# Gate tiles between the pool pairs, an earlier weight block in the last scan group, and single PSUM banks for one product

## The chip, the core and the metric

The kernel runs on one NeuronCore of a Trainium2 chip. The metric is the device time of one execution in microseconds (us). The engines are PE (TensorE, matrix products; PEld is its weight load), DVE (VectorE, elementwise), ACT (ScalarE, elementwise and activation functions), POOL (GpSimd, here only for issuing DMAs) and SP (which issues most DMAs from its queue). Matrix products are written to PSUM, an accumulator memory of eight banks of 128 x 512 floats; all other on-chip data lie in SBUF.

## The reference

One layer of a decoder trunk on 512 tokens with 16 meta tokens ahead of them, model width 1024. Cut to what the change touches:

```python
u = rmsnorm(h, mix_norm_w)                      # 528 x 1024
proj = u @ w_in
gates = sigmoid(proj[..., OFF_GATE:] + b_gate)  # 2 x 1024 columns
gate_pool, gate_ssd = gates[..., :1024], gates[..., 1024:]
y_pool = pool_mixer(u_pool, pool_w_group, pool_scale) @ w_pool_up
y_ssd = mamba2_branch(z, xbc, dt_raw, ...) @ w_ssd_out
h = h + (gate_pool * y_pool + gate_ssd * y_ssd) @ w_o
v = rmsnorm(h, mlp_norm_w)
h = h + square(relu(v @ w_ff1)) @ w_ff2
out = rmsnorm(h, final_norm_w)
```

`pool_mixer` takes, in four groups of 256 channels, the mean over the last 2, 4, 8 or 16 positions minus the value itself, multiplies each group by a 256 x 256 matrix and scales it. `mamba2_branch` is a chunked scan in eight groups of 256 channels.

## The kernel before

Precision. The float32 products are made of products in a reduced format: each factor is split into a high part (a cast on ACT) and a low part (original minus high, on DVE), and three products are added in PSUM: high x high, high x low, low x high. `block()` loads one weight block of 128 x 1024 from a packed array (through one of three `raw` buffers), casts it to `whi` (L87) and subtracts to `wlo` (L88); there are four buffers of each. `mm3s` (L119, L120, L122) makes the three products of a list of factor pairs: first, pair by pair, high weight with high and low data, then the low weights. `proj` (L183, L185) does the same for eight pieces of 128 rows of `w_in`.

Order. Each engine works through its own queue in a fixed order, set when the program is built: a planner models the time and gives each engine, of the instructions whose inputs it takes to be ready, the one that was written earliest. So a step written earlier has precedence, and a step can be drawn ahead of others to fill a gap in the modelled time. `tc.issue_after(x)` holds an instruction behind x on its engine. The planner also deals out buffers: `psum2` takes one of two buffers of two banks (pool `psa`), `psum1` one of four single banks (pool `psb`). Weight blocks are loaded in the order in which `_weight_blocks` packs them, which must match the order in which the kernel asks for them.

The scan. `ssd(g)` handles scan group g as a generator of steps: transposes and the differences for the decay mask (L496 on ACT, L499 on DVE); chunk states `st` (L519 to L529) and the masked decay `abc` (exponentials L502, L503 on ACT, mask L530 on DVE); for each half the outputs `po` (state part) and `py` (masked part), and the DVE work on y (L546 to L550); squares; the norm; the final scaling with the split of y into `yh` and `yl` (L571, L572). `weave` alternates these steps with those of other generators. For the last group, g = 7, the other generator is `out_part`, which multiplies y of groups 4 to 6 (`ys[8]` to `ys[13]`) by pieces of `w_ssd_out` into `psp` and adds the sum to `acc` (L647). `PARTS` gives its order: for output tiles d = 0 and 1 first k = 8 to 11, later k = 12 and 13 (which come from group 6, the group just finished), then d = 2 to 7 whole. Its weights come by a generator `pieces` that gets a block (L634, L636) when its first piece is asked for; block 0 serves the first parts of d = 0 and 1, block 1 the late parts of both and the first four pieces of d = 2.

The pool branch. Behind the scan, `pool_tile` computes the two tiles of pool group 3; then eight products `psl` (k = 14, 15, the last group's y) are added to `acc` (L814 to L817); then comes one gate tile of the pool branch (`gate_pool(NK - 1)`). Pool groups 2, 1 and 0 are each computed by `pool_pair(p)` (L735 to L784): seven products of a split-matrix scheme with four weight forms A, S, D, B made from two raw blocks on DVE (sums L741 to L745, splits L105 and L106), into `pxx` (two banks), `py` and `pz` (single banks). `averaged` (L714) takes the windowed means on DVE, `pooled_halves` (L726) splits them, and `pool_mix(g)` multiplies by the group matrix into `pg`, scales and splits into `yph`, `ypl` (L796, L797). A pair is written ahead of the mix of the pair before.

The merge. For each of the eight output tiles d in the order of `MERGE`, `gate_ssd(d)` computes a gate tile (24 matmuls into `pgs`, a sigmoid L805 into one of two `gt` buffers); the product `pup` multiplies the pooled parts by `w_pool_up` (L926); `acc` is multiplied by the gate (L927) and the products added. Before the change the first gate tile is written behind pair 0 and in front of the mix of group 0; in the merge loop each turn first makes the gate tile of the next turn.

Of the kernel before, what the change touches and what calls it, by code (L numbers as in the profile page):

```python
# [9 lines left out]
F32 = mybir.dt.float32  # L10
F32R = mybir.dt.float32r
AF = mybir.ActivationFunctionType
ALU = mybir.AluOpType

P = 128
D = 1024
SEQ = 512
# [3 lines left out]
NK = D // P  # L21
G = 8
# [35 lines left out]
def kernel(ctx: ExitStack, tc, xT, x, w, vec, fnw, out):  # L58
# [12 lines left out]
    def block_tiles():  # L71
        b = nblk[0]
        nblk[0] += 1
        return (b, wp.tile([P, 1024], F32, tag="raw", name=f"raw{b}", bufs=3),
                wp.tile([P, 1024], F32R, tag="whi", name=f"whi{b}"),
                wp.tile([P, 1024], F32R, tag="wlo", name=f"wlo{b}"))

    def block_load(t, c):
        nc.sync.dma_start(t[1][:, c], w[t[0], :, c])
# [36 lines left out]
    def mm3s(ps, pairs, first=True, last=True):  # L116

        for n, ((ah, al), (bh, bl)) in enumerate(pairs):
            pe.matmul(ps, ah, bh, start=first and n == 0, stop=False)  # L119
            pe.matmul(ps, ah, bl, start=False, stop=False)  # L120
        for n, ((ah, al), (bh, bl)) in enumerate(pairs):
            pe.matmul(ps, al, bh, start=False, stop=last and n == len(pairs) - 1)  # L122
# [39 lines left out]
    def psum2(name):  # L162
        return psa.tile([P, 1024], F32, tag="mm", name=name)
# [51 lines left out]
    b = nblk[0]  # L215
# [409 lines left out]

    def out_part():

        def pieces():
            for n in range(6):
                t = block_tiles()  # L630
                block_load(t, slice(0, 1024))

                with tc.issue_after(b_meta[G - 1].ins) if n == 1 else nullcontext():
                    act.copy(t[2], t[1])  # L634
                with tc.issue_after(x_decayed[G - 1].ins) if n == 1 else nullcontext():
                    dve.tensor_tensor(t[3], t[1], t[2].bitcast(F32), op=ALU.subtract)  # L636
                for j in range(NK):
                    c = slice(j * P, (j + 1) * P)
                    yield t[2][:, c], t[3][:, c]

        un, ps = pieces(), {}
        for d, ks in PARTS:
            if d not in ps:
                ps[d] = psum2(f"psp{d}")[:, :SEQ]
            mm3s(ps[d], [(next(un), ys[k]) for k in ks], ks[0] == 8, ks[-1] == 13)
            if ks[-1] == 13:
                dve.tensor_tensor(acc[d], acc[d], ps[d], op=ALU.add)  # L647
            yield


# [135 lines left out]
    def pool_mix(gi, pooled, wgb):  # L786
        ps = [psum1(f"pg{gi}_{j}") for j in range(2)]
        wh, wl = wgb
        for j in range(2):
            os = [(gi % 2) * 512 + k * 256 + j * P for k in range(2)]  # L790
            mm3s(ps[j], [((wh[:, o : o + P], wl[:, o : o + P]), pooled[k]) for k, o in enumerate(os)])
        for j in range(2):
            t = 2 * gi + j
            h = yp.tile([P, SEQ], F32R, tag="yh", name=f"yph{t}")
            l = yp.tile([P, SEQ], F32R, tag="yl", name=f"ypl{t}")
            act.activation(h, ps[j], AF.Copy, scale=col(V_PS, t))  # L796
            dve.scalar_tensor_tensor(l, ps[j], col(V_PS, t), h.bitcast(F32),  # L797
                                     op0=ALU.mult, op1=ALU.subtract)
            yps[t] = (h, l)
# [12 lines left out]

    un = units()
    for d in range(NK):  # L814
        ps = psum2(f"psl{d}")[:, :SEQ]
        mm3s(ps, [(next(un), ys[k]) for k in (14, 15)])
        dve.tensor_tensor(acc[d], acc[d], ps, op=ALU.add)  # L817
    wgb = block()
    gate_pool(NK - 1)
    for n, gi in enumerate(POOL_ORDER):  # L820
        if n == 0:
            pool_mix(gi, pend, wgb)
            nxt = pool_pair(POOL_ORDER[1])
            continue
        pend, nxt = nxt, pool_pair(POOL_ORDER[n + 1]) if n < 3 else None
        if n == 2:
            wgb = block()
        if n == 3:
            gts = [gate_ssd(MERGE[0])]

        pend = [pooled_halves(*a, copied[POOL_ORDER[n + 1]] if n < 3 else None) for a in pend]
        with tc.issue_after(last[POOL_ORDER[n + 1]].ins) if n < 3 else nullcontext():
            pool_mix(gi, pend, wgb)
    pool_stack.close()
    wo_stack = ExitStack()
    wop = wo_stack.enter_context(tc.tile_pool(name="wop", bufs=1, side="right", reuse_waits="tile"))
# [77 lines left out]
    ks = [2 * gi + i for gi in POOL_ORDER for i in range(2)]  # L914
    first = []
    for n, d in enumerate(MERGE):
        if n + 1 < NK:
            gts.append(gate_ssd(MERGE[n + 1]))
        if n >= NK - 2:
            first.append(split(woq["b11", n - NK + 2]))  # L920
        ps = psum2(f"pup{d}")[:, :SEQ]
        wh, wl = block()
        if n < len(WO_ORDER):
            wo_load(*WO_ORDER[n])
        cs = [slice(k * P, (k + 1) * P) for k in ks]
        mm3s(ps, [((wh[:, c], wl[:, c]), yps[k]) for c, k in zip(cs, ks)])  # L926
        dve.tensor_tensor(acc[d], acc[d], gts[n], op=ALU.mult)  # L927
        dve.tensor_tensor(m1[d], m1[d], ps, op=ALU.mult)
        dve.tensor_tensor(acc[d], acc[d], m1[d], op=ALU.add)
        factors(d)  # L930
# [325 lines left out]
def _weight_blocks(i):  # L1256

    w_in, w_g, w_up = i["w_in"][0], i["pool_w_group"][0], i["w_pool_up"][0]
    w_so, w_o, f1, f2 = i["w_ssd_out"][0], i["w_o"][0], i["w_ff1"][0], i["w_ff2"][0]
    blocks = []  # L1260

    def cols(m, c):
        a = m[:, c : c + P]
        return a.reshape(NK, P, P).transpose(1, 0, 2).reshape(P, NK * P)

    def put(b):
        blocks.append(b)

    wdt = w_in[:, OFF_DT : OFF_DT + HEADS].reshape(NK, P, HEADS).transpose(1, 0, 2).reshape(P, NK * HEADS)
    put(np.concatenate([wdt, np.zeros((P, 1024 - NK * HEADS), wdt.dtype)], 1))  # L1270

    def group(g, gate_d=None):
        for t in (16 + g, 24 + g, 2 * g, 2 * g + 1):
            put(cols(w_in, OFF_XBC + t * P))
        if gate_d is not None:
            gate(gate_d)
        for j in range(2):
            put(cols(w_in, OFF_Z + (2 * g + j) * P))

    def wg(b):  # L1280
        put(w_g[2 * b : 2 * b + 2].reshape(2, 2, P, 256).transpose(2, 0, 1, 3).reshape(P, 1024))

    def gate(d):
        put(cols(w_in, OFF_GATE + d * P))

    def pieces(parts):

        u = [w_so[k * P : (k + 1) * P, d * P : (d + 1) * P] for d, ks in parts for k in ks]
        return [np.concatenate(u[j : j + NK], 1) for j in range(0, len(u), NK)]

    group(0)
    for d in range(GATES_FIRST):
        gate(d)
    for g in range(G - 1):
        if g == 4:
            for d in range(NK):
                put(cols(w_so[:D], d * P))
        group(g + 1, GATE_AT.get(g))
    blocks += pieces(PARTS)
    for t in range(2):  # L1300
        put(cols(w_in, (2 * POOL_ORDER[0] + t) * P))
    blocks += pieces([(d, (14, 15)) for d in range(NK)])
    wg(POOL_ORDER[0] // 2)
    gate(NK - 1)
    for n in range(4):
        for k in ((1, 2) if n == 0 else (n + 2,) if n == 1 else ()):
            for i in range(2):
                put(cols(w_in, (2 * POOL_ORDER[k] + i) * P))
        if n == 3:
            gate(NK + MERGE[0])  # L1310
        if n == 2:
            wg(POOL_ORDER[n] // 2)

    def wo(name, i):
        put(rows(w_o, 2 * (name[1] == "2") + i, int(name[2] == "2")))

    def rows(m, k2, half):
        a = m[k2 * 2 * P : (k2 + 1) * 2 * P, half * 512 : (half + 1) * 512]
        return a.reshape(2, P, 512).transpose(1, 0, 2).reshape(P, 1024)

    for n, d in enumerate(MERGE):
        if n + 1 < NK:
            gate(NK + MERGE[n + 1])
        put(cols(w_up, d * P))
        if n < len(WO_ORDER):
            wo(*WO_ORDER[n])
    for i in range(2):
        wo("b21", i)

    def quarter(c, k, half):  # L1330

        a = [f2[(4 * c + 2 * p + k) * P : (4 * c + 2 * p + k + 1) * P, half * 512 : (half + 1) * 512]
             for p in range(2)]
        return np.concatenate(a, 1)

    def quarters(c):
        for k, half in ((1, 0), (1, 1), (0, 1), (0, 0)):
            put(quarter(c, k, half))

    ff = list(range(32))  # L1340

    def ff1():
        if ff:
            put(cols(f1, ff.pop(0) * P))

    for _ in range(6):
        ff1()
    for c in range(8):
        quarters(c)
        for _ in range(3 if c > 4 else 4):  # L1350
            ff1()
    return np.ascontiguousarray(np.stack(blocks))
# [38 lines left out]
```

## Time and profile before

| | us |
|---|---|
| median of 3 runs | 1017.9 (1017.82 to 1017.94) |
| profiled execution | 1017.53 |
| its span, first to last instruction | 1015.8 |
| PE busy in the span | 1004.9 |
| DVE busy | 763.5 |
| ACT busy | 561.7 |

Times in timelines are microseconds from the start of the span. A row of a timeline has the start, the duration, the engine, the line, the operation, what is written and read, the shape, and the number of instructions merged into the row; idle time of the engine ahead of it and what ended it stand in brackets. A row of the waits has the engine and line that waited, the engine and line that ended the wait, the total in us, the number of times and the longest. In the busy time by stage each row has the window, its length, then for PE, PEld, DVE, ACT and POOL the busy time and the number of instructions, then the granted PE clock, the share of DMA and the rate. The matmuls are pipelined: one row of a 512-column product lasts 0.39 us, while the next one starts 0.23 us after it.

### The profile page before, as it was taken

How to read it: one execution, taken by the hardware profiler on the slowest of the kernel's cores; microseconds unless marked ns; L12 is line 12 of the kernel's file. 1: busy time of each engine (PE TensorE's matmuls, PEld its weight loads, DVE VectorE, ACT ScalarE, POOL GpSimd, SP SyncE). 2: the span in 40 equal slices, each digit the busy share in tenths (PEclk: the TensorE clock that was granted, in tenths of full speed). 3: DMA queues.
4: the chain of work that ended last, by engine and by line, in shares of the span. 5: the costliest groups of instructions: out<-in, count | busy, mean ns of one | idle time of the engine just before them, and what ended most of it. 6: DMA issues, size and time to landing. Idle time of an engine off the chain costs nothing.

```text
span 1015.8 us, 14212 instructions
## 1 busy us (share of the span) xinstructions
PE 1004.9 (99%) x5661; PEld 866.4 (85%) x5661; DVE 763.5 (75%) x1039; ACT 561.7 (55%) x748; POOL 35.9 (4%) x72
## 2 busy tenths in 40 slices
PE   9999999999999999999999999999999999999997
PEld 8889899999889999978898888888888888888886
DVE  7988798877746587787888557887676686676866
ACT  8665958586727349563256333465545455354444
POOL 0010000101000000012000001000000000000000
PEclk9999999999999999999999999999999999999999
DMA  7272143616233231428125534133333323324112
GB/s 250 80 245 107 63 145 106 220 46 194 80 97 135 83 131 38 146 65 272 60 83 196 178 97 153 42 118 131 104 101 107 104 83 125 102 85 125 42 42 83
DMA packets 35602, 118.41 MB, mean 117 GB/s; under 512 B 4112, under 2 KB 5456, under 8 KB 34512
## 3 DMA queue, kind: packets, MB, share of 16 engines
q1 hardware_dynamic: 26928, 92.75, 28.6%
q0 software_dynamic: 7888, 23.86, 6.9%
q8 instruction: 44, 0.72, 0.3%
q10 hardware_dynamic: 720, 0.91, 0.2%
q14 instruction: 22, 0.18, 0.1%
HBM read 108.94 MB, written 8.55 MB: 116 GB/s over the span
## 4 chain that ended last, share of the span: by engine, by line
PE 93%; DVE 5%; ACT 1%; DMA 1%; issue 1%; DVEq 0%; ACTq 0%
PE px L183 11%; PE alpha L1141 6%; PE pf L120 6%; PE pf L119 6%; PE pf L122 6%; PE px L185 6%; PE pz L183 5%; PE alpha L1144 3%; PE pgp L183 3%; PE pgs L183 3%; PE pz L185 3%; PE py L543 2%; PE pso L119 2%; PE pgp L185 1%; PE wo_alpha L958 1%; PE pso L120 1%
## 5 line engine op out<-in xcount | busy, mean ns | idle before, releaser
L87 ACT CAST whi<-raw 128x1024 fp32r<-128x1024 f32 (+2 forms) x122 | 124.1, 1023 | 175.7 <-PE pf L120 47.0
L88 DVE TENSOR_TENSOR wlo<-raw,whi 128x1024 fp32r<-128x1024 f32 (+2 forms) x122 | 144.0, 1186 | 96.2 <-ACT whi L87 70.9
L183 PE MATMUL px<-uh,whi 128*128 128x264 f32 (+1 forms) x448 | 113.2, 291 | 0.0
L185 PE MATMUL px<-ul,whi 128*128 128x264 f32 (+1 forms) x448 | 110.5, 285 | 0.0
L119 PE MATMUL pf<-vh,whi 128*128 128x512 f32 x256 | 99.8, 390 | 0.0
L120 PE MATMUL pf<-vl,whi 128*128 128x512 f32 x256 | 99.6, 389 | 0.0
L183 PEld LDWEIGHTS px<-uh,whi 128*128 128x128 f32 x448 | 84.6, 189 | 1.8 <-issue 1.4
L185 PEld LDWEIGHTS px<-ul,whi 128*128 128x128 f32 x448 | 84.2, 188 | 0.4 <-issue 0.2
L905 DVE TENSOR_TENSOR slo<-b,shi 128x1024 fp32r<-128x1024 f32 x35 | 42.7, 1220 | 28.8 <-ACT shi L904 15.2
L122 PE MATMUL pf<-vh,wlo 128*128 128x512 f32 x256 | 63.6, 389 | 0.0
L904 ACT CAST shi<-b 128x1024 fp32r<-128x1024 f32 x35 | 36.8, 1051 | 44.8 <-PE pf L120 30.2
L183 PE MATMUL px<-uh,wlo 128*128 128x264 f32 (+1 forms) x448 | 58.5, 283 | 0.0
L122 PEld LDWEIGHTS pf<-vh,wlo 128*128 128x128 f32 x256 | 48.1, 188 | 10.0
L119 PEld LDWEIGHTS pf<-vh,whi 128*128 128x128 f32 x256 | 48.1, 188 | 9.9
L120 PEld LDWEIGHTS pf<-vl,whi 128*128 128x128 f32 x256 | 48.0, 188 | 9.9
L183 PEld LDWEIGHTS px<-uh,wlo 128*128 128x128 f32 x448 | 55.9, 188 | 0.0
L1141 PE MATMUL alpha<-shi,hh 128*128 128x512 f32 x140 | 54.6, 390 | 0.0
L1144 PE MATMUL alpha<-shi,hl 128*128 128x512 f32 x140 | 54.5, 389 | 0.0
L971 DVE TENSOR_TENSOR ht<-ht,alpha 128x1024 f32<-128x1024 f32 x35 | 42.6, 1218 | 15.7 <-PE alpha L1141 15.7
L185 PE MATMUL pz<-ul,whi 128*128 128x512 f32 x112 | 43.6, 389 | 0.0
L183 PE MATMUL pz<-uh,whi 128*128 128x512 f32 x112 | 43.6, 389 | 0.0
L564 DVE RECIPROCAL rs<-rs 128x128 f32<-128x128 f32 x32 | 27.2, 909 | 13.7 <-ACT rs L562 13.6
(497 smaller groups left out, 2423.6 us busy)
## 6 DMA issues: line engine op xcount, KB each, us to landing
raw<-in_w SPq DMA_DIRECT2D x128, 512.0 KB, 3.6
b<-in_w SPq DMA_DIRECT2D x28, 512.0 KB, 3.6
abc<-acs_d POOLq DMA_DIRECT2D x8, 1024.0 KB, 6.3
wob<-in_w SPq DMA_DIRECT2D x8, 512.0 KB, 5.3
xt<-in_xT SPq DMA_DIRECT2D x8, 264.0 KB, 4.9
u_d<-xt POOLq DMA_DIRECT2D x8, 260.0 KB, 2.8
ht<-in_x POOLq DMA_DIRECT2D x4, 512.0 KB, 5.6
w<-in_w SPq DMA_DIRECT2D x4, 512.0 KB, 3.5
```

The costliest lines, as they stand in the source:

```text
L87: act.copy(hi[:, c], raw[:, c])
L88: dve.tensor_tensor(lo[:, c], raw[:, c], hi[:, c].bitcast(F32), op=ALU.subtract)
L119: pe.matmul(ps, ah, bh, start=first and n == 0, stop=False)
L120: pe.matmul(ps, ah, bl, start=False, stop=False)
L122: pe.matmul(ps, al, bh, start=False, stop=last and n == len(pairs) - 1)
L183: pe.matmul(o, wt, rhs[0][k][:, c], start=part == 0 and k == 0, stop=part == 1 and k == NK - 1)
L185: pe.matmul(o, wt, rhs[1][k][:, c], start=False, stop=False)
L904: act.copy(hi, src)
L905: dve.tensor_tensor(lo, src, hi.bitcast(F32), op=ALU.subtract)
L971: dve.tensor_tensor(o, o, src, op=op)
L1141: pe.matmul(ps[t], hh[:, p, seg, st], m, start=bool(first and not low and p == 0), stop=bool(last and low and p == 1), skip_group_check=True)
L1144: pe.matmul(ps[t], hl[:, p, seg, st], m, start=False, stop=False, skip_group_check=True)
```

## The change

Three edits.

First, `out_part`: the first two weight blocks are both got at its first step. The late parts of d = 0 and 1 are no longer two steps of `mm3s`, one for each d, each followed by its add to `acc`, but three steps: high x high for both d, then low weight x high y for both, then high weight x low y for both; the two adds stand behind these, at the beginning of the step that computes d = 2.

Second, the eight `psl` products use single banks (`psum1`) in place of the two-bank buffers.

Third, two gate tiles of the merge move. That of `MERGE[0]` is written behind the pair of group 1 and ahead of the halves and the mix of group 2, and so ahead of the pair of group 0 too. That of `MERGE[1]`, so far the first step of the merge loop, is written behind the pair of group 0 and the mix of group 1, ahead of the mix of group 0. The first turn of the merge loop then has no gate tile, and the first `pup` product follows the mix of group 0. The packed weight blocks are put in the new order; the number of blocks, of matmuls and of elementwise instructions stays.

```diff
     def out_part():
 
+        def get(n):
+            t = block_tiles()
+            block_load(t, slice(0, 1024))
+
+            with tc.issue_after(b_meta[G - 1].ins) if n == 1 else nullcontext():
+                act.copy(t[2], t[1])
+            with tc.issue_after(x_decayed[G - 1].ins) if n == 1 else nullcontext():
+                dve.tensor_tensor(t[3], t[1], t[2].bitcast(F32), op=ALU.subtract)
+            return t
+
         def pieces():
+            blocks = [get(0), get(1)]
             for n in range(6):
-                t = block_tiles()
...
+                t = blocks[n] if n < 2 else get(n)
                 for j in range(NK):
                     c = slice(j * P, (j + 1) * P)
                     yield t[2][:, c], t[3][:, c]
 
-        un, ps = pieces(), {}
-        for d, ks in PARTS:
-            if d not in ps:
-                ps[d] = psum2(f"psp{d}")[:, :SEQ]
-            mm3s(ps[d], [(next(un), ys[k]) for k in ks], ks[0] == 8, ks[-1] == 13)
-            if ks[-1] == 13:
-                dve.tensor_tensor(acc[d], acc[d], ps[d], op=ALU.add)
+        un = pieces()
+
+        def part(ps, d, ks):
+            mm3s(ps, [(next(un), ys[k]) for k in ks], ks[0] == 8, ks[-1] == 13)
+
+        def add(ps, d):
+            dve.tensor_tensor(acc[d], acc[d], ps, op=ALU.add)
+
+
+        ps = [psum2(f"psp{d}")[:, :SEQ] for d in range(2)]
+        for d in range(2):
+            part(ps[d], d, range(8, 12))
+            yield
+        late = [[(next(un), ys[k]) for k in (12, 13)] for d in range(2)]
+        for o in ((0, 0), (1, 0), (0, 1)):
+            for d in range(2):
+                for n, (a, b) in enumerate(late[d]):
+                    pe.matmul(ps[d], a[o[0]], b[o[1]], start=False, stop=o[1] == 1 and n == 1)
+            yield
+        for d in range(2):
+            add(ps[d], d)
+        for d in range(2, NK):
+            ps = psum2(f"psp{d}")[:, :SEQ]
+            part(ps, d, range(8, 14))
+            add(ps, d)
             yield
...
     for d in range(NK):
-        ps = psum2(f"psl{d}")[:, :SEQ]
+        ps = psum1(f"psl{d}")
         mm3s(ps, [(next(un), ys[k]) for k in (14, 15)])
         dve.tensor_tensor(acc[d], acc[d], ps, op=ALU.add)
     wgb = block()
     gate_pool(NK - 1)
-    for n, gi in enumerate(POOL_ORDER):
-        if n == 0:
-            pool_mix(gi, pend, wgb)
-            nxt = pool_pair(POOL_ORDER[1])
-            continue
-        pend, nxt = nxt, pool_pair(POOL_ORDER[n + 1]) if n < 3 else None
+    pool_mix(POOL_ORDER[0], pend, wgb)
+    nxt = pool_pair(POOL_ORDER[1])
+    gts = []
+    for n in range(1, 4):
+        pend, ahead = nxt, None
+        if n < 3:
+            nxt, ahead = pool_pair(POOL_ORDER[n + 1]), POOL_ORDER[n + 1]
         if n == 2:
             wgb = block()
-        if n == 3:
-            gts = [gate_ssd(MERGE[0])]
-
-        pend = [pooled_halves(*a, copied[POOL_ORDER[n + 1]] if n < 3 else None) for a in pend]
-        with tc.issue_after(last[POOL_ORDER[n + 1]].ins) if n < 3 else nullcontext():
-            pool_mix(gi, pend, wgb)
+        else:
+            gts.append(gate_ssd(MERGE[len(gts)]))
+
+        pend = [pooled_halves(*a, copied.get(ahead)) for a in pend]
+        with tc.issue_after(last[ahead].ins) if n < 3 else nullcontext():
+            pool_mix(POOL_ORDER[n], pend, wgb)
...
     for n, d in enumerate(MERGE):
-        if n + 1 < NK:
+        if 0 < n < NK - 1:
             gts.append(gate_ssd(MERGE[n + 1]))
```

More of the change, by code (lines that the diff above doesn't have):

```diff
@@ L626, in out_part @@
     def out_part():
+        def get(n):
[6 more added lines that the diff above has]
+            return t
         def pieces():
+            blocks = [get(0), get(1)]
             for n in range(6):
-                t = block_tiles()
[L631 to L636, printed above, removed]
+                t = blocks[n] if n < 2 else get(n)
                 for j in range(NK):
@@ L1305, in _weight_blocks @@
     for n in range(4):
-        for k in ((1, 2) if n == 0 else (n + 2,) if n == 1 else ()):
+        if n < 3:
             for i in range(2):
-                put(cols(w_in, (2 * POOL_ORDER[k] + i) * P))
-        if n == 3:
-            gate(NK + MERGE[0])
+                put(cols(w_in, (2 * POOL_ORDER[n + 1] + i) * P))
+        if n % 2:
+            gate(NK + MERGE[n // 2])
         if n == 2:
@@ L1321, in _weight_blocks @@
     for n, d in enumerate(MERGE):
-        if n + 1 < NK:
+        if 0 < n < NK - 1:
             gate(NK + MERGE[n + 1])
```

## The prediction

> **What bounds the kernel now.** I read the page first, then busy time by stage around the lines that the change touches, then the waits.
>
> ```profile
> span 1015.8 us, 14212 instructions
> PE 1004.9 (99%) x5661; PEld 866.4 (85%) x5661; DVE 763.5 (75%) x1039; ACT 561.7 (55%) x748; POOL 35.9 (4%) x72
> PEclk9999999999999999999999999999999999999999
> ```
> ```profile
> 444.00:454.00 10.00, 8.29 (x63) 6.46 (x63) 9.89 (x15) 4.01 (x5) 0.36 (x1) 1.00 0.30 77
> ...
> 490.00:510.00 20.00, 19.82 (x90) 16.10 (x89) 16.18 (x24) 6.66 (x8) 0.00 (x0) 1.00 0.08 27
> 510.00:534.00 24.00, 23.77 (x187) 23.00 (x186) 21.23 (x33) 11.18 (x20) 0.00 (x0) 1.00 0.28 89
> 534.00:546.00 12.00, 10.76 (x82) 9.96 (x81) 11.04 (x18) 6.68 (x12) 0.00 (x0) 1.00 0.24 85
> 546.00:640.00 94.00, 94.00 (x416) 77.70 (x415) 60.68 (x83) 36.00 (x48) 2.66 (x5) 1.00 0.49 168
> ```
>
> The PE is the bound: 1004.9 of 1015.8 us, at full clock. The columns of the second view are PE, PEld, DVE, ACT, POOL, then clock. Only two stretches lose PE time worth speaking of: 444 to 454 (1.71 us idle, DVE busy 9.89 of 10) and 534 to 546 (1.24 us idle, DVE busy 11.04 of 12). Behind 546 the PE has no idle time at all. The change removes and adds no matmul, so it can only win or lose waits of the PE.
>
> ```profile
> PE psp L119 <- ACT whi L634: 1.7, 1, 1.7
> PE pdt L225 <- DVE ones_r L130: 1.5, 1, 1.5
> PE pxx L764 <- DVE wloS L106: 1.1, 1, 1.1
> PE pxx L764 <- DVE pu L778: 0.2, 1, 0.2
> PE psl L119 <- DVE acc L817: 0.2, 1, 0.2
> ```
> ```profile
> PEld psp L119 <- ACT whi L634: 1.9, 1, 1.9
> ...
> PEld psp L119 <- DVE acc L647: 0.6, 1, 0.6
> ...
> PEld psl L119 <- DVE acc L817: 0.6, 1, 0.6
> ...
> PEld pxx L764 <- DVE wloS L106: 1.3, 1, 1.3
> ...
> PEld pxx L764 <- DVE pu L778: 0.4, 1, 0.4
> PEld pxx L764 <- ACT whiD L105: 0.3, 1, 0.3
> PEld pxx L764 <- DVE wloD L106: 0.2, 1, 0.2
> ```
>
> The waits at the lines of the change, on the PE itself, sum to 1.7 + 1.1 + 0.2 + 0.2 = 3.2 us (1.5 us more lies at the kernel's start). The waits of the weight load in the same places sum to 5.3 us: a matmul's row is longer than its pace, so a short wait hides under the row before it. What can be won lies between 3.2 and 5.3 us; the question is how much comes back elsewhere.
>
> [...] By busy time alone the pair term below would be 1.2 instead of 1.8, and my sum 0.6 us smaller.
>
> **A: the second weight block one step ahead (scan group 7).**
>
> ```profile
> 443.84 0.61 PE L537 MATMUL po<-ct,st 128*128 128x128 f32 x4
> 446.15 0.50 PE L119 MATMUL psp<-yh,whi 128*128 128x512 f32 x1 [1.71 <-ACT whi L634]
> ...
> 448.20 0.65 PE L543 MATMUL py<-abc,xdt 128*64 128x128 f32 x6
> ...
> 453.26 0.50 PE L119 MATMUL psp<-yh,whi 128*128 128x512 f32 x1
> ```
> ```profile
> 437.88 1.85 ACT L496 ACTIVATE abc<-abc,dtok 128x128 f32<-128x128 f32 x6
> 440.44 0.37 ACT L523 COPY st<-pst 128x256 f32<-128x256 f32 x1 [0.70 <-PE pst L521]
> ...
> 443.09 1.12 ACT L571 CAST yh<-yt 128x512 fp32r<-128x512 f32 x2
> 444.11 1.05 ACT L503 ACTIVATE abc<-abc 128x1024 f32<-128x1024 f32 x1
> 445.07 2.94 ACT L634 CAST whi<-raw 128x1024 fp32r<-128x1024 f32 x3
> ```
> ```profile
> 443.72 1.29 DVE L572 TENSOR_TENSOR yl<-yt,yh 128x512 fp32r<-128x512 f32 x2 [0.80 <-ACT yh L571]
> ...
> 445.87 2.28 DVE L530 TENSOR_TENSOR abc<-abc,cbm 128x2048 f32<-128x2048 f32 x1
> ...
> 448.40 1.22 DVE L636 TENSOR_TENSOR wlo<-raw,whi 128x1024 fp32r<-128x1024 f32 x1
> ...
> 451.34 0.68 DVE L647 TENSOR_TENSOR acc<-acc,psp 128x512 f32<-128x512 f32 x1
> ...
> 457.05 1.33 DVE L647 TENSOR_TENSOR acc<-acc,psp 128x512 f32<-128x512 f32 x2
> ```
>
> The PE stands at 444.4 until the second block's cast, the first of the three at 445.07, is done at 446.1. That cast lies behind both exponentials of the decay. Written one step earlier it is free to run once the six L496 are through, at 439.7, in the 0.70 us that ACT waits for the states; it takes 2.94 / 3 = 0.98 us, so everything behind it on ACT (state copy, table load, decay, yh casts, L503) slips by some 0.3 us. The yh casts then end at 444.2 + 0.3 = 444.5, and the late products start there instead of at 446.15.
>
> But py is next, and py waits for the mask L530, which ends at 448.15 now and with ACT's 0.3 us at about 448.5. Today 8 of the 12 late products fill 446.15 to 448.09; in the new order all 12 run at 0.23 us each (gate rows below), 2.7 us, 444.5 to 447.2. No other product can start: the two sums hold both of the wide PSUM buffers. So the PE waits again, 447.2 to 448.5. Old wait 1.7 us, new waits 0.1 + 1.3 = 1.4: the direct gain is 0.3 us. With the second block's wlo (1.22 us, at 448.40 now) gone from behind the mask, the adds can take its place, and the wait of the weight load for the acc add (0.6 us, of which I count 0.4) goes. Sum for A: 0.3 + 0.4 = **0.7 us**. Bounds: if the cast lands behind the state copy, ACT slips by 0.98 us, the mask ends at 449.1, the new wait grows by 0.6 and A gives 0.1; if wlo falls into DVE's 0.80 us of idle time and neither ACT's slip nor wlo moves the mask, the products run from 444.2 to 446.9, the new wait is 1.2 us, and with the whole 1.9 and 0.6 of the weight loads gone A gives 1.3. The order of the adds is the second rival.
>
> **B: single banks for the psl products.** Eight products of six matmuls move from the two wide buffers to the four single banks. The one wait this can remove is psl on acc L817, 0.2 us on the PE and 0.6 on the weight load; I take **0.4**. Nothing else uses more than two of those banks between 490 and 510 (pg), so at worst psl has two, as now: 0 to 0.6.
>
> **C: a gate tile between pair 1 and pair 0, and one behind pair 0.**
>
> ```profile
> raw<-in_w SPq DMA_DIRECT2D x128, 512.0 KB, 3.6
> ```
> ```profile
> 548.48 0.39 PE L183 MATMUL pgs<-uh,whi 128*128 128x512 f32 x1
> ...
> 553.92 0.39 PE L119 MATMUL pg<-ph,whi 128*128 128x512 f32 x1
> ...
> 556.64 0.39 PE L183 MATMUL pgs<-uh,whi 128*128 128x512 f32 x1
> ...
> 558.53 0.68 ACT L796 ACTIVATE yph<-pg,vs 128x512 fp32r<-128x512 f32 x1
> ...
> 559.81 0.74 DVE L797 SCALAR_TENSOR_TENSOR ypl<-pg,vs,yph 128x512 fp32r<-128x512 f32 x1
> ```
>
> A gate tile is 24 matmuls, 548.48 to 553.92 = 5.44 us, 0.227 each. The first moves from behind pair 0 to ahead of it. Pair 0 stalls because DVE (21.23 busy of 24, then 11.04 of 12) delivers its wloS, wloD late; the moved tile gives DVE 5.44 us of PE time and takes one wlo (1.22) and one add onto acc (0.7) with it, so 3.5 us of cover remain, and the late ones are late by 1.3, 0.3 and 0.2. All 1.8 us go, plus the slower first matmul after each stall, some 0.1 each (0.50 and 0.39 us rows after waits): **2.0 us**. Ends: 0.9 if half of the stalls stay, because DVE's queue spends the cover on work that stands behind pair 0's forms today (mix and halves of the pairs before); 2.6 if the 0.4 on L778 and its restart go as well; they lie inside pair 1, ahead of the moved tile, and I leave them.
>
> What is late next. In SP's queue the gate's block goes ahead of pair 0's two blocks and takes a raw buffer that was theirs; a load lands 3.6 us after its issue, under the 5.44. The gate's whi and wlo take the slot of pair 1's S form, free after the fourth of that pair's seven products, and pair 0's D form gets the gate's. Cost 0; with that cover gone, what the 3.6 us exceed of the remaining 3.5, so 0.1, and if two loads queue, 3.7.
>
> The second gate tile now lies between the mixes of pairs 1 and 0, and the first pup product follows the last mix at once. Today a gate tile (from 556.64) covers the chain from that mix to ypl, which ends at 559.81 + 0.74 = 560.55, 3.9 us behind the mix. In the new order 12 matmuls (6 of 8 inputs, 2.7 us) come before the first that needs it, and two more before the last ypl is used; the bare chain is 0.68 + 0.68 + 0.74, 2.1 us. I count 0; at today's length it costs 3.9 - 2.7 - 0.5 = 0.7 us. The sigmoids and gate buffers (two) are the same in number, and the third gate tile waits only for the product with acc, which is ready early.
>
> **Sum.** 0.7 + 0.4 + 2.0 = 3.1 us. The profiled execution took 1017.53 us with a span of 1015.8, 0.37 below the median of 1017.9; 1017.53 - 3.1 = 1014.4, and against the median 1017.9 - 3.1 = **1014.8 us**.
>
> **The rivals**, in times against the median; what can be told from no change here is 0.2%, 2.0 us.
>
> 1. *The waits move.* A gives 0.1 (mask 1 us later) and the exposed mix costs 0.7, while C holds: 0.1 + 0.4 + 2.0 - 0.7 = 1.8, 1016.1 us. For it: DVE is busy 9.89 of 10 us in A, so any wait removed on ACT ends at DVE. Against: the ACT gap of 0.70 us is there to take the cast. Chance 0.2.
> 2. *Slower: the two acc adds fall behind the scan's y.* They are now written after the squares' step, so eight DVE instructions on y, which fill DVE from 452.1 to 457.05, come first wherever the order was made as if the late products ended later. Then the third psp product can't have its PSUM buffer until 457.7 instead of 453.26: 4.4 us more, A gives 0.7 - 4.4 - 0.4 = -4.1, and the whole -4.1 + 2.4 = -1.7: 1019.6 us. It decides once the first add starts later than 452. Against: the late products end near 447, five us ahead of that. Chance 0.1.
> 3. *Pair 0 is late again.* DVE is the bound from 510 to 546, and the added wlo stands ahead of pair 0's forms, whose buffers free later: C gives 0.9, total 2.0, 1015.9 us. For: DVE's share. Against: 3.5 us of cover for stalls of at most 1.3. Chance 0.12.
> 4. *All of it goes*: A 1.3, B 0.6, C 2.6, 4.5 us: 1013.4. Chance 0.1.
>
> [...]
>
> **How the numbers follow.** The forecast has 0.48 (gains of 2.1 to 4.2), the rivals 0.2, 0.1, 0.12 and 0.1. Faster by over 0.2% means below 1015.9: the forecast, rival 4 and a third of rival 3, 0.62. Within 0.2%: rival 1, two thirds of rival 3 and a little of rival 2, 0.31. Slower, above 1019.9: rival 2 is priced 0.3 us short of that and the fourth psp product would wait as well, so I put 0.07 of its 0.1 there. The range takes in rival 4 and stops short of rival 2: from 1013.0 to 1017.4 (a gain of 4.9 to one of 0.5).
>
> **What would show it.** A: L634's second cast near 440, the first late psp product near 444.5, a new PE wait on the mask L530 of about 1.3 us, psp adds ahead of the y instructions. B: no wait of psl. C: no PE wait on wloS in pair 0, a gate tile ahead of it, no wait of pup on ypl. I am wrong if the late products wait for yl or wlo in front of py, if the third psp product starts after 453, or if DVE's lateness reaches the gate tile itself.

## The result, and the profile after

| | before | after |
|---|---|---|
| median, 6 runs each (us) | 1017.92 (1017.0 to 1018.55) | 1013.01 (1012.3 to 1013.75) |
| profiled execution | 1017.53 | 1013.65 |

The changed kernel is faster by 4.9 us, 0.9952 of the time before (95% interval 0.994 to 0.9965). The forecast was 1014.8, a gain of 3.1: the time lies 0.01 us inside the fast end of the range, nearest to rival 4 (1013.4). The first three fences are of the kernel after: the busy row of its page (span 1012.0 us), its busy time by stage (columns as before: PE, PEld, DVE, ACT, POOL, clock), and the one wait of the PE in the stages of the change.

```profile
PE 1002.7 (99%) x5661; PEld 866.4 (86%) x5661; DVE 763.4 (75%) x1039; ACT 561.9 (56%) x748; POOL 35.8 (4%) x72
```
```profile
444.00:454.00 10.00, 9.10 (x59) 7.37 (x57) 10.00 (x16) 5.41 (x7) 0.00 (x0) 1.00 0.23 57
490.00:510.00 20.00, 20.00 (x94) 16.74 (x94) 16.57 (x25) 7.74 (x9) 0.00 (x0) 1.00 0.13 44
510.00:534.00 24.00, 24.00 (x182) 23.03 (x182) 21.36 (x34) 10.34 (x17) 0.00 (x0) 1.00 0.31 96
534.00:546.00 12.00, 12.00 (x90) 11.42 (x89) 11.07 (x17) 7.90 (x13) 0.00 (x0) 1.00 0.24 77
```
```profile
PE py L543 <- PE psp L663: 0.9, 1, 0.9
```

Of the stages that the change touches, only 444 to 454 still has idle PE time, 0.90 us, and the second fence's other rows have none. The waits on `whi` L634, `wloS`, L778 and L817 are gone; one new wait of 0.9 us stands in front of `py`.

Where the time came from can be read from start to start, which a matmul's modelled end doesn't blur. Each fence has the start of group 7's transposes (`ptb`), of the first product behind the scan (`pp`), of the first `psl` and of the first `pup` product, and of the last product of the kernel (`last`), before and then after.

```profile
433.74 0.49 PE L464 MATMUL ptb<-ident,bt 128*128 128x128 f32 x3
...
478.84 0.28 PE L183 MATMUL pp<-uh,whi 128*128 128x264 f32 x1
...
490.50 0.39 PE L119 MATMUL psl<-yh,whi 128*128 128x512 f32 x1
...
562.08 0.39 PE L119 MATMUL pup<-yph,whi 128*128 128x512 f32 x1
...
1009.80 0.28 PE L1243 MATMUL last<-shi,hl 128*128 128x256 f32 x1
```
```profile
435.02 0.49 PE L464 MATMUL ptb<-ident,bt 128*128 128x128 f32 x3
...
478.16 0.28 PE L183 MATMUL pp<-uh,whi 128*128 128x264 f32 x1
...
489.82 0.40 PE L119 MATMUL psl<-yh,whi 128*128 128x512 f32 x1
...
558.22 0.39 PE L119 MATMUL pup<-yph,whi 128*128 128x512 f32 x1
...
1005.93 0.28 PE L1267 MATMUL last<-shi,hl 128*128 128x256 f32 x1
```

The scan group (A) went from 478.84 - 433.74 = 45.10 to 43.14 us, the stretch from `psl` to `pup` (B and C) from 71.58 to 68.40: 1.96 + 3.18 = 5.1 us. The profiled execution of after reached group 7 at 435.02, 1.28 us later than the one of before, ahead of everything that was changed; that is why the two profiled times differ by only 3.9.

**The scan group, after.** PE, ACT and DVE in the timeline of after:

```profile
445.25 1.17 PE L663 MATMUL psp<-yh,whi 128*128 128x512 f32 x4
...
447.78 0.71 PE L663 MATMUL psp<-yl,whi 128*128 128x512 f32 x2
449.39 1.09 PE L543 MATMUL py<-abc,xdt 128*64 128x128 f32 x16 [0.90 <-PE psp L663]
450.41 1.16 PE L537 MATMUL po<-ct,st 128*128 128x128 f32 x8
451.33 0.48 PE L119 MATMUL psp<-yh,whi 128*128 128x512 f32 x1
```
```profile
440.92 1.03 ACT L633 CAST whi<-raw 128x1024 fp32r<-128x1024 f32 x1
```
```profile
442.13 1.16 DVE L635 TENSOR_TENSOR wlo<-raw,whi 128x1024 fp32r<-128x1024 f32 x1
...
446.99 2.29 DVE L530 TENSOR_TENSOR abc<-abc,cbm 128x2048 f32<-128x2048 f32 x1
...
449.53 0.69 DVE L652 TENSOR_TENSOR acc<-acc,psp 128x512 f32<-128x512 f32 x1
```

Subtract 1.28 from these times to lay them beside those of before. The second block's cast runs at 440.92 (439.64), straight behind the six L496, and its `wlo` at 442.13, right behind the reciprocals; the 0.80 us for which DVE stood idle in front of `yl` are gone. The late products start at 445.25 (443.97, before 446.15). The waits put the 0.90 us in front of `py` down to the PE's own `psp`; that product had ended 0.90 us before, and what ends last is the mask: 446.99 + 2.29 = 449.28, and `py` starts at 449.39. The adds follow at 449.53 and 450.46, ahead of the y instructions, and the third psp product starts at 451.33 (450.05, before 453.26).

**The pool pairs, after.** PE, then DVE:

```profile
527.51 0.39 PE L183 MATMUL pgs<-uh,whi 128*128 128x512 f32 x1
527.76 0.39 PE L787 MATMUL pxx<-t42h,whiB 128*128 128x260 f32 x1
...
541.09 0.64 PE L787 MATMUL pxx<-t42h,wloS 128*128 128x260 f32 x4
```
```profile
536.39 1.23 DVE L106 TENSOR_TENSOR wloS<-sm,whiS 128x1024 fp32r<-128x1024 f32 x1
...
560.19 0.74 DVE L820 SCALAR_TENSOR_TENSOR ypl<-pg,vs,yph 128x512 fp32r<-128x512 f32 x1
```

Pair 0's `wloS` is ready at 536.39 + 1.23 = 537.62 and first used at 541.09, 3.5 us in reserve where it was 1.1 us late. One matmul of the gate tile (527.51) has been drawn into pair 1, in front of the product with B, where the PE used to wait for L778 (of the weight load's 0.4 us there, 0.2 are left). At the end the last `ypl` is ready at 560.93, 2.7 us behind the first `pup` product, and no `pup` product waits.

### The profile page after: what moved, and what is told of

It is laid out like the page before. It is cut to its first block, busy times and chain, and to the rows that moved or that the text cites. A ratio compares the mean times of both kernels' runs of the same rounds, so it can differ in the third digit from the quotient of the medians.

```text
span 1012.0 us, 14216 instructions
## 1 busy us (share of the span) xinstructions
PE 1002.7 (99%) x5661; PEld 866.4 (86%) x5661; DVE 763.4 (75%) x1039; ACT 561.9 (56%) x748; POOL 35.8 (4%) x72
## 4 chain that ended last, share of the span: by engine, by line
PE 96%; DVE 2%; DMA 1%; ACT 0%; issue 0%; SPq 0%; ACTq 0%
PE px L183 11%; PE alpha L1165 6%; PE pf L120 6%; PE pf L122 6%; PE pf L119 6%; PE px L185 6%; PE pz L183 5%; PE alpha L1168 3%; PE pgp L183 3%; PE pgs L183 3%; PE pz L185 3%; PE py L543 2%; PE pso L119 2%; PE po L537 1%; PE pso L120 1%; PE pgp L185 1%
```

## The experiments

Ratios are to the kernel before, with 95% intervals, against runs of it on the same chip; its medians there were 1017.73, 1017.96, 1017.84 and 1017.67 us.

Part of the scatter lies ahead of all edits: in the profiled executions of these runs group 7's first transpose starts between 433.56 and 435.02 us, though nothing before it differs. From that transpose on, stretches that an edit leaves alone repeat within 0.15 us. So the table gives each gain over the kernel before twice, in us: by the medians, and in the trace, from that transpose to the start of the last product (576.06 us before; one profiled execution each). For small differences the trace is the better measure.

| run | by the medians | in the trace |
|---|---|---|
| all three edits | 4.9 | 5.15 |
| first edit alone | 2.2 | 1.99 |
| second edit alone | 0.6 | 0.59 |
| third edit alone | 2.2 | 2.63 |
| first gate tile alone | 2.0 | 1.96 |
| all, both gate tiles ahead of pair 0 | 4.7 | 4.76 |
| no windowed sums of group 2 | 0.6 | 0.70 |
| no windowed sums, one load less | 2.5 | 2.57 |
| early block alone | 2.2 | 2.12 |
| passes and later adds alone | -7.0 | -7.25 |
| all, second block's `wlo` on POOL | 3.7 | 3.60 |
| all, two sums to one buffer | 5.8 | 5.58 |
| the same, late parts as two steps | 5.6 | 5.61 |

### The three edits one at a time

*The first edit alone* (the scan group as in the change, all else as before):

```diff
+            blocks = [get(0), get(1)]
...
+        for o in ((0, 0), (1, 0), (0, 1)):
+            for d in range(2):
...
+        for d in range(2):
+            add(ps[d], d)
```

> Only the change in the last scan group is made (early second block, late parts in three passes, later adds); the psl banks and the gate tiles stay as before. By the trace of the changed kernel this stretch, from group 7's first transpose to the first pool product, went from 45.1 to 43.1 us, so if the edits act apart from one another the time falls by about 1.9 us, to 1016.0. By the size on record (0.7 us) it would be 1017.2. If the time won here were lost again in the pool stage, where DVE sets the pace, it would be 1017.9.

Measured: 1015.55 us, 0.998 [0.9972, 0.9989], a gain of 2.2 us.

*The second edit alone:*

```diff
-        ps = psum2(f"psl{d}")[:, :SEQ]
+        ps = psum1(f"psl{d}")
```

> Only the psl products move to single banks. Theory: the one wait for the add onto acc goes, 0.4 us, 1017.5, and no PE wait on L817 is left in the trace. Rival: the PE then only waits for pair 2's forms instead, 1017.9.

Measured: 1017.13 us, 0.9993 [0.9984, 1.0001]. By the times alone it can't be told from no change; in the trace 0.59 us are gone, and the stage from 490 to 510, which had 0.18 us of idle PE time, has none.

*The third edit alone:*

```diff
+        else:
+            gts.append(gate_ssd(MERGE[len(gts)]))
...
-        if n + 1 < NK:
+        if 0 < n < NK - 1:
```

> Only the two gate tiles move; scan group and psl banks as before. Theory: all waits inside pairs 1 and 0 go, 2.0 us by the prediction, 2.7 by the changed kernel's trace with the psl wait taken off: 1015.2 to 1015.9, and no PE wait on wloS or wloD. Rival (pair 0 late again, DVE the bound): 1017.0.

Measured: 1015.53 us, 0.9975 [0.9965, 0.9985], a gain of 2.2 us. The three gains, 2.2 + 0.6 + 2.2 = 5.0, are the 4.9 of all of them, and in the trace 1.99 + 0.59 + 2.63 = 5.21 stand against 5.15: the edits don't help or hinder one another.

### Which gate tile does the work

The first gate tile moved as in the change, the second left in the merge loop:

```diff
+        if n == 1:
+            gts.append(gate_ssd(MERGE[0]))
...
     for n, d in enumerate(MERGE):
         if n + 1 < NK:
```

> From the kernel before, only the first gate tile moves ahead of pair 0; the second stays in the first turn of the merge loop, so nothing is written between the mixes of groups 1 and 0. Theory: pair 0 has its cover, but the mix of group 0 now comes up right behind the mix of group 1 while its halves are still being averaged on DVE, and the PE, which takes its queue in order, waits there some 2 us: 1017 or a little over. Rival: the first gate tile is all that matters, and the second one is drawn forward by itself: 1015.2 to 1015.9 as with both.

Measured: 1015.77 us, 0.998 [0.9972, 0.9989], 0.24 us more than with both tiles moved, and 0.67 us more in the trace. I had expected a stall of some 2 us in front of the mix of group 0, and this fell. The PE rows at that place:

```profile
551.79 0.39 PE L120 MATMUL pup<-ypl,whi 128*128 128x512 f32 x1
552.42 0.74 PE L119 MATMUL pg<-ph,whi 128*128 128x512 f32 x2 [0.24 <-ACT ph L731]
```

The planner laid `pup` products whose inputs were ready, and matmuls of the next gate tile, between those of the last mix; what is left is a wait of 0.24 us of the PE, and 0.7 us of the weight load. The first tile removes pair 0's stalls alone; the second is worth 0.67 us.

The other way round, both tiles ahead of pair 0:

```diff
-        else:
-            gts.append(gate_ssd(MERGE[len(gts)]))
+        if n == 1:
+            gts += [gate_ssd(MERGE[0]), gate_ssd(MERGE[1])]
```

> The changed kernel with both gate tiles ahead of pair 0, 10.9 us of PE time in place of 5.4, and none between the mixes of groups 1 and 0. Theory: one tile covers DVE fully, so the second brings nothing in pair 0, and the mix of group 0 loses its cover as with the first gate alone: 0.5 to 0.7 us more, 1013.6. Rival: DVE is still the bound behind pair 1 and more cover brings more, 1012.5 or less.

Measured: 1013.22 us, 0.9953 [0.994, 0.9965], against 1013.01 for the change: twice the cover gains nothing more in pair 0, since no stall is left there. Of the 0.5 to 0.7 us that I expected to lose at the last mix, 0.2 show in the medians and 0.39 in the trace.

### Why pair 0 was late

The kernel before with the windowed sums of pool group 2 (L720) left out, some 3.7 us of DVE time ahead of pair 0's forms:

```diff
-        while wdt < win:
+        while wdt < win and t // 2 != 2:
```

> The kernel before, with the windowed sums of pool group 2 left out (six additions on DVE, some 3.7 us, between the forms of pairs 1 and 0). Nothing else moves: psl and gates as before. Theory: pair 0's stalls come from DVE's load, so they go here too: no PE wait on wloS, wloD and whiD in pair 0, the stretch from the first pair product to the last falls from 35.5 to 33.5 us or less, the time to about 1015.9. Rival: pair 0's forms wait for buffers and loads, which this leaves as they are: 35.5 us.

Measured: 1017.23 us, 0.9995 [0.9986, 1.0004]. Taking the load off DVE gave little, 0.70 us in the trace. A wait of the PE, one of SP's queue and two DVE rows of this run:

```profile
PE pxx L764 <- DVE wloS L106: 0.5, 1, 0.5
```
```profile
SPq L99 <- DVE wloD L106: 8.6, 1, 8.6
```
```profile
522.92 1.22 DVE L106 TENSOR_TENSOR wloD<-raw,whiD 128x1024 fp32r<-128x1024 f32 x1
...
527.76 0.69 DVE L741 TENSOR_TENSOR sm<-raw 128x512 f32<-128x512 f32 x1 [2.53 <-DMA raw<-in_w]
```

With 3.7 us less to do, DVE came to pair 0's first sum early and stood there 2.53 us for the second raw block to land. The load of that block had itself waited 8.6 us in SP's queue for a raw buffer: it was issued at 524.20, when pair 1's `wloD` had ended on DVE (522.92 + 1.22 = 524.14), and landed some 3.6 us later. In the kernel before it is the same: `wloD` ends at 522.60, the load is issued at 522.63, and DVE begins the sum at 526.25. So neither theory held as it was put: DVE's queue and the landing of that block set the same point in time, and the landing follows an earlier instruction of DVE, which this edit did not bring forward.

To tell them apart, the same kernel with pair 0 computing with its first raw block in place of its second, so that one load less is made:

```diff
-        a1, a2 = raw_block(), raw_block()
+        a1 = raw_block()
+        if p == 0:
+            nblk[0] += 1
+        a2 = raw_block() if p else a1
```

> The kernel before with the windowed sums of pool group 2 left out (as in the run before this one) and, further, pair 0 computing with its first raw block in place of its second, so that the load of that block is left out. Theory: pair 0 is late for two causes that stand in series, VectorE's load and the late load of the second raw block; with both gone TensorE no longer waits for wloS or wloD in pair 0, the stretch from the first to the last product of the pool matmuls falls from 34.7 to about 33.5 us, and the run is 1015.9 us. Rival: the stalls that are left come from the order in which the pair's casts and subtractions are placed; then the stretch stays at about 34.7 us and the time at 1017.2 us.

Measured: 1015.19 us, 0.9977 [0.9966, 0.9988].

```profile
534.00:546.00 12.00, 12.00 (x91) 11.48 (x91) 11.59 (x19) 7.41 (x12) 0.00 (x0) 1.00 0.40 121
```
```profile
529.84 1.22 DVE L106 TENSOR_TENSOR wloS<-sm,whiS 128x1024 fp32r<-128x1024 f32 x1
```

`wloS` runs at 529.84 instead of 537.22, the PE idles nowhere in this stage, and the gain, 2.57 us in the trace, is that of the gate tiles (2.63). With DVE's load alone gone the block was late; with both gone the stalls are gone. The run with the late load removed and DVE's load kept was not made, so whether the load by itself would have been enough is not shown.

### Which part of the first edit does the work

The second block got early, the late parts and adds as two steps as before:

```diff
+            blocks = [get(0), get(1)]
...
+        for d in range(2):
+            part(ps[d], d, range(12, 14))
+            add(ps[d], d)
+            yield
```

> The scan's early second block alone: late parts in the old form (high and low y together, then low weights, one d after the other, each followed by its add), psl and gates as before. The stretch from group 7's first transpose to the first pool product is 45.1 us in the kernel before and 43.1 with the whole scan edit. Theory: the early block brings the products forward, but each d's second product needs yl, and the PE then meets the mask all the same; about half of the gain, 44.1 us, 1016.7. Rival: the early block is the whole edit, 43.1 us, 1015.7.

Measured: 1015.81 us, 0.9979 [0.997, 0.9987], the same as the whole first edit (1015.55; 2.12 and 1.99 us in the trace), where I had expected half. Its PE waits in the scan group:

```profile
PE py L543 <- PE psp L122: 0.4, 1, 0.4
PE psp L120 <- DVE yl L572: 0.2, 1, 0.2
```

What was one wait in front of `py` is here a shorter one and another for `yl`. The opposite half, three passes and the adds behind them, without the early block:

```diff
             for n in range(6):
-                t = block_tiles()
...
+                t = get(n)
...
+        for o in ((0, 0), (1, 0), (0, 1)):
+            for d in range(2):
...
+        for d in range(2):
+            add(ps[d], d)
```

> The three passes and the later adds alone: the second block is got when its first piece is asked for, as before. Theory: the cast again lies behind the decay's exponentials, the PE waits for it 1.7 us as before, and the stretch stays near 45.1 us, 1017.7. Rival: the order of the passes and of the adds is what counts, 43.1 us, 1015.7.

Measured: 1024.98 us, 1.0074 [1.006, 1.0088], 7.0 us slower by the medians. The waits, the busy time by stage, the PE and DVE of this run:

```profile
PE psp L119 <- DVE acc L651: 4.0, 1, 4.0
PE psp L662 <- ACT whi L633: 1.7, 1, 1.7
...
PE py L543 <- DVE abc L530: 0.9, 1, 0.9
```
```profile
456.50:457.00 0.50, 0.00 (x0) 0.00 (x0) 0.50 (x1) 0.00 (x0) 0.36 (x1) 0.79 1.26 387
```
```profile
458.30:463.60 5.30, 5.25 (x11) 3.48 (x12) 3.69 (x5) 3.27 (x5) 1.07 (x2) 0.50 0.74 218
```
```profile
453.83 0.50 PE L662 MATMUL psp<-yl,whi 128*128 128x512 f32 x1
458.35 0.79 PE L119 MATMUL psp<-yh,whi 128*128 128x512 f32 x1 [4.02 <-DVE acc L651]
458.94 0.63 PE L120 MATMUL psp<-yl,whi 128*128 128x512 f32 x1
459.37 0.63 PE L119 MATMUL psp<-yh,whi 128*128 128x512 f32 x1
```
```profile
457.61 1.28 DVE L651 TENSOR_TENSOR acc<-acc,psp 128x512 f32<-128x512 f32 x2
```

This is the prediction's second rival, at the place and time that it named: the adds start at 457.61, behind the eight DVE instructions on y, and the third psp product waits 4.0 us for their PSUM buffer. The 1.7 us on the cast stay, and 0.9 us on the mask come on top. And the granted clock falls to half while the PE stands: from 458.35 to 463.60 a 512-column product takes 459.37 - 458.94 = 0.43 us instead of 0.23, so about half of those 5.25 us, 2.6, is lost to the clock; from 463.60 to 468.00 it is 1.00 again. 4.0 + 0.9 + 2.6 = 7.5, less the 0.4 of the old wait for the add: 7.1, where 1024.98 - 1017.96 = 7.0 were measured (7.25 in the trace). The passes win nothing of their own, and it is the early block that keeps the adds ahead of y.

### Can DVE be relieved, or the last wait filled?

The second block's `wlo` on POOL instead of DVE, the rest as in the change:

```diff
-                dve.tensor_tensor(t[3], t[1], t[2].bitcast(F32), op=ALU.subtract)
+                (pool if n == 1 else dve).tensor_tensor(t[3], t[1], t[2].bitcast(F32), op=ALU.subtract)
```

> The changed kernel with the second block's wlo subtraction on POOL, which does nothing else there, in place of DVE. Theory: what is left of the PE's wait (0.9 us in front of py) is DVE's, since the mask comes behind that subtraction of 1.16 us; with it gone the mask ends 1.1 us earlier, the wait falls to 0.1 or less, the stretch from 43.1 to about 42.2 us, the time to 1012.1. Rival: the mask is set by ACT's exponential, and the wait stays. If POOL takes over 4 us for 128x1024, the products of the low weights wait for it and the time rises by what exceeds that.

Measured: 1014.28 us, 0.9963 [0.995, 0.9975], 1.3 us above the change, 1.55 in the trace; my theory fell. POOL and DVE of this run:

```profile
441.06 2.40 POOL L635 TENSOR_TENSOR wlo<-raw,whi 128x1024 fp32r<-128x1024 f32 x1 [23.14 <-ACT whi L633]
```
```profile
441.28 2.46 DVE L528 TENSOR_TENSOR st<-st,cdec 128x256 f32<-128x256 f32 x1
...
445.92 0.41 DVE L528 TENSOR_TENSOR st<-st,cdec 128x256 f32<-128x256 f32 x1
```

POOL needs 2.40 us where DVE needs 1.16, and a DVE instruction of 0.41 us that began 0.22 us behind it took 2.46. DVE lost 2.05 us to be spared 1.16, and the mask ends 16.02 us behind group 7's first transpose instead of 14.26.

The sums of two output tiles in one two-bank buffer, so that the sums of d = 2 and 3 find a buffer free while those of d = 0 and 1 are still open:

```diff
-        ps = [psum2(f"psp{d}")[:, :SEQ] for d in range(2)]
+        def two(d):
+            t = psum2(f"psp{d}")
+            return [t[:, :SEQ], t[:, SEQ:]]
+
+        ps = two(0)
...
+            if d % 2 == 0:
+                ps = two(d)
+            part(ps[d % 2], d, range(8, 14))
+            add(ps[d % 2], d)
```

> The changed kernel, with two psp sums to one wide buffer (one in each half), so that d = 2 and 3 have the second buffer free while the PE waits in front of py; the planned order of the PE then has nine products of d = 2 ahead of py. Theory: what is left of the wait (0.9 us, 1.06 from start to start) is a lack of other products, not of time on DVE; it goes, the stretch of the scan falls from 43.1 to 42.1 us, and the time to 1012.0. Rival: the products that are drawn forward need the third block's cast or another y and wait there; 43.1 us and 1013.0.

Measured: 1012.07 us (1011.99 to 1012.2), 0.9942 [0.993, 0.9955], the fastest by the medians, 0.9 us below the change; in the trace the two are 0.43 us apart. The PE of this run, and a wait of its weight load:

```profile
448.11 0.39 PE L119 MATMUL psp<-yh,whi 128*128 128x512 f32 x1
...
449.34 1.09 PE L543 MATMUL py<-abc,xdt 128*64 128x128 f32 x16
```
```profile
PEld psp L119 <- DVE acc L652: 0.6, 1, 0.6
```

Products of d = 2 now run from 448.11, while the mask is made, and `py` follows without a wait of the PE. But a later sum, at 459.52, waits for an add again, 0.6 us of the weight load, as one did in the kernel before: about half of the expected 1.0 us was won. The same with the late parts as two steps, each with its add:

```diff
-        for o in ((0, 0), (1, 0), (0, 1)):
...
+        for d in range(2):
+            part(ps[d], d, range(12, 14))
+            add(ps[d], d)
             yield
-        for d in range(2):
-            add(ps[d], d)
```

> The same with the late parts in their old form (no passes, adds right behind). Theory: the passes bring nothing beside the early block, as in the run of the early block alone, so the stretch is the same within 0.1 us, 42.1, and the time 1012.0. Rival: with other products in the gap the products that need yl stall the queue, 0.2 to 0.4 us more.

Measured: 1012.25 us, 0.9944 [0.9931, 0.9958], in the trace 0.03 us faster: the passes make no difference here either.

## Why the prediction was right, and where its sizes were off

**A, forecast 0.7, measured 2.2 by the medians and 1.96 in the trace.** The mechanism was right in its order: cast in ACT's gap, late products some 2 us earlier, then a new wait of the PE for the mask, adds ahead of y. The term "the direct gain is 0.3 us" was mis-sized, for two reasons. First, it let the mask slip by ACT's 0.3 us. It ends 449.28 - 435.02 = 14.26 us behind group 7's first transpose, before 445.87 + 2.28 - 433.74 = 14.41: the mask follows DVE's own queue, and that had 0.80 us of idle time, which took up most of the new `wlo` (1.16). This is the case that the prediction gave as the upper bound. In waits of the weight load, 1.9 (cast) and 0.6 (add) went and this one came:

```profile
449.36 0.88 PEld L543 LDWEIGHTS py<-abc,xdt 128*64 128x64 f32 x16 [1.30 <-PE psp L663]
```

That is 1.9 + 0.6 - 1.3 = 1.2 us. (The old first `py`, at 448.20, had waited for the mask too; it started 0.34 us behind the product before it, where 0.23 is the pace, so 0.1 us more went there.) Second, the prediction priced waits alone and left out what the order itself costs. In the kernel before, `py` and `po` were laced together:

```profile
448.78 0.49 PE L537 MATMUL po<-ct,st 128*128 128x128 f32 x2
449.20 0.87 PE L543 MATMUL py<-abc,xdt 128*64 128x128 f32 x10
450.00 0.71 PE L537 MATMUL po<-ct,st 128*128 128x128 f32 x4
```

From start to start, the 16 `py` took (448.78 - 448.20) + (450.00 - 449.20) = 1.38 us and the two `po` 0.42. After the change the 16 `py` in one run take 450.41 - 449.39 = 1.02, and eight `po` 0.92, 0.115 each. That is 0.36 + 0.19 = 0.55 us, which I put down to fewer changes between the two shapes; no run changed these alone. With the 1.2 and the 0.1 it makes 1.85 of the 1.96.

**B, forecast 0.4, measured 0.6** by the median, with an interval that reaches no change, and 0.59 in the trace, the upper end of its 0 to 0.6. The wait that it named went.

**C, forecast 2.0, measured 2.2 by the medians and 2.63 in the trace**, where the prediction gave 2.6 as the upper end. "All 1.8 us go" held: the stages from 510 to 546 have no idle PE time. The prediction left the 0.4 us on L778 aside because it lies ahead of the moved tile; the planner drew one gate matmul in front of it (527.51 above), and that wait went from the PE too. The second tile at no cost held; that its absence costs 0.67 us, not a stall of 2, was seen only by the run without it. What the prediction had incompletely is the cause of pair 0's lateness. It said that DVE delivers late because it is busy; the run without the windowed sums shows that the landing of pair 0's second raw block sets the same time, through the buffer that pair 1's `wloD` holds. The gate tile gives time to both, so the sum didn't suffer; an edit that had relieved DVE alone would have been priced at up to 1.8 us and have given 0.7.

**The rivals.** Of the first, the waits did move, but to a shorter one (1.3 of the weight load against 2.5). The second did not come true in the change, where the first add starts at 449.53, and is real: the run without the early block is it, with 4.0 us where 4.4 were worked out. Behind that wait the PE also ran at a granted clock of 0.50, from 458.30 to 463.60, by my estimate 2.6 us more. The third is excluded by the rows of 534 to 546. The fourth, A 1.3, B 0.6, C 2.6, is what happened, with A larger still.

The forecast was right in sign and in the waits that go, and short by 1.8 us by the medians and by 2.05 in the trace, of which A has 1.3, C 0.6 and B 0.2. The terms came out at their upper ends (B, C) or beyond (A), and the range holds the result only because it was drawn to take in rival 4, whose chance was put at 0.1. That the median lies 0.01 us inside it and not outside is luck, since single executions went from 1012.3 to 1013.75.

## What to carry to other kernels

Count the wait of the weight load, the first matmul after it (0.50 us in the row at 446.15 of the kernel before, where those behind it last 0.39 to 0.40) and, by my estimate 0.55 us in A, the changes between shapes, not only the idle time of the PE: the waits of the busy column gave A 0.3 us, start to start it was 2. When a step's input is late, ask which of its inputs is late next, down to the load of the raw data and the instruction that frees the buffer for that load, before an engine is relieved. When part of the scatter lies ahead of an edit, compare traces from a mark behind that part. And an instruction that frees a PSUM buffer is worth a look at what can be queued ahead of it: the same two adds cost nothing at 449.5 and, at 457.6, 4.0 us of waiting and 2.6 at half clock.

## What the runs showed of the hardware

Behind a wait of 4.0 us the PE ran at half clock, by my estimate 2.6 us more. In the run with the passes alone the last product ends at 454.33. The granted clock is 1.00 from 454.00 to 456.50, 0.79 as a mean from 456.50 to 457.00 and 0.50 from 457.00 to 458.00, so it fell near 456.8, 2.5 us into the idle time. It came back at 463.6 (a mean of 0.69 from 463.00 to 464.00), 5.2 us behind the start of the next product at 458.35: some 6.8 us at half clock. The delay was not the same everywhere. At the end of the span, where the PE has no work either, the last product ends at 1009.80 + 0.28 = 1010.08 in the kernel before and at 1005.93 + 0.28 = 1006.21 after the change; the means of 0.80 from 1013.50 to 1014.00 and of 0.77 from 1009.00 to 1009.50 put the fall of the clock 3.7 and 3.1 us behind it. In the kernel before, the wait of 1.71 us left the clock at 1.00. What sets the delay is not shown.

A DVE instruction beside one on POOL took 2.46 us, where another of the same line and shape took 0.41. It began at 441.28, 0.22 us behind the POOL instruction (441.06), and ended at 443.74, 0.28 us behind the end of that one (441.06 + 2.40 = 443.46). One pair of instructions shows it here, and no run shows the cause.
